# One softmax split into near keys and keys of one residue modulo 4, in a transformer block on one core

## The chip, the core and the metric

The kernel runs on one core of a Trainium2 chip. A core has TensorE (PE, matrix products into PSUM, with a weight load, PEld, ahead of each product), VectorE (DVE), ScalarE (ACT), GpSimd (POOL), and SyncE (SP), whose queue issues nearly all DMAs of this kernel. Each engine works through its own instructions in order and waits on semaphores for the others. The metric is the device time of one launch in microseconds, lower being better.

## The reference, cut to what matters

One block over 1024 tokens of 1024 channels in float32: normalization, one input projection, a gated convolution branch of width 31, an attention branch with 16 heads of 64, gates that mix both, an output projection, and a feed-forward part with a convolution of width 3. The attention is what the change rewrites:

```python
DILATION_GROUPS = ((128, 1), (512, 4), (2048, 16))
...
    for window, dilation in DILATION_GROUPS:
        o_g, lse_g = dilated_window_attention(q, k, v, slopes, window, dilation)
        outs.append(o_g)
        lses.append(lse_g)
    mix = jax.nn.softmax(jnp.stack(lses), axis=0)
    o = jnp.einsum('gbsh,gbshd->bshd', mix, jnp.stack(outs))
```

Each of the three groups attends causally within its window to keys at distances that are multiples of 1, 4 or 16, with a penalty that grows with distance (one slope a head). Mixing three softmaxes by their log-sums equals one softmax over all keys in which a key counts once for each group that holds it. So for a query only these keys have weight: all at distances 0 to 128, and beyond that those at multiples of 4 (up to 512) and of 16 (to the start). Beyond 128, every key that counts has the query's residue modulo 4.

## The kernel before, in words

Each float32 operand of a product is split into a high and a low part (`split`, lines 74 to 77: ScalarE copies the high part, VectorE subtracts it), and a product is three matmuls of the parts, or two where one operand carries both halves in its partitions.

The work runs in stages. Stage 1 (lines 197 to 342) loads x in eight tiles of 128 consecutive tokens (line 204), normalizes and transposes them, computes the two GLU halves by channel (`apad`, line 237), runs the 31-tap convolution on VectorE (`conv_branch`) beside the q, k and v products on TensorE, and spills q, k, v and the gates to DRAM. The gates' products (`gate_steps`, line 146) are a generator; a part of them covers the end of the convolution (`COVER`).

Stage 2 (lines 345 to 470) is the attention. `head` fetches one head's q, k (high and low), v and its row of the mask, all in rings of two buffers. For each block of 128 queries, `score` multiplies q with all keys up to the block's end (128 to 1024 columns), VectorE adds the mask and takes the row extreme in one operation (line 389), ScalarE takes the exponential with its row sum (391), VectorE the reciprocal (392), and GpSimd scales the row (393). `flip` transposes the probabilities by blocks of 128 keys on TensorE, and `weigh` multiplies v with them. `step` runs the scores of one half of a head beside the weighing of the half before, and `fill` pulls steps of side work from `side_work` in between, at rates set by `FILL`: a step is three matmuls of 512 columns. The side work is what is left of the gates and then the convolution branch's output product (`ya`). It has 256 + 128 such steps in all.

Stage 3 (from line 474) loads the attention's output from DRAM (`load_split(oT, do_, ...)`, line 477), multiplies it (`yb`), mixes with gates and `ya` (`merge`), and goes on to the output projection and the feed-forward part, which the change leaves alone.

The order of each engine's instructions is fixed when the program is built: a scheduler plays the program with modelled times, in the priority of the text, and writes down a sequence for each engine. On the chip the sequences stand as written.

The lines that the prediction names: 190 (transposes of x), 204, 221 to 224, 237, 261 and 322 (the end of the convolution), 374 (mask), 384 and 385 (scores), 389 to 393, 400 (transposes of probabilities), 408 and 409 (weighing), 451 to 456 (sum of both halves of the output and its store), 485 to 487 (loads of stage 3).

## Time and profile before

| | |
|---|---|
| median of 3 runs | 1814.08 us (1813.51 to 1816.09) |
| profiled execution | 1811.43 us, span 1809.6 us |
| TensorE clock granted, mean | 0.991 |
| instructions | 22474, of these 8244 matmuls |
| TensorE, VectorE, ScalarE, GpSimd busy | 98%, 73%, 43%, 11% of the span |
| DMA | 257.57 MB in 142063 packets |
| first score to last side work | 549.6 to 976.4 us |

The profile is of one execution, and its busy shares are averages over stages with different limits, so the prediction reads it by stretches. Matmuls overlap, and a busy TensorE is judged better by how far apart its products start than by their durations. A row of a group has its line, engine, operation, output and inputs, count, busy time and mean duration, then the idle time before it and what ended that. A row of a DMA has its median time from issue to landing.

### The profile page before, as it was taken

The page shows a single profiled execution, that of the slowest core. Times are in us where ns is not written, and L with a number is a line of the kernel's source. Part 1 is how long each engine was busy: PE and PEld are TensorE (multiplying, and loading weights), DVE is VectorE, ACT ScalarE, POOL GpSimd, SP SyncE. Part 2 cuts the span into 40 slices and gives each one's busy share as a digit, 9 for nine tenths or more (in the row PEclk, how much of TensorE's full clock was granted, in tenths as well). Part 3 has the DMA queues.
Part 4 walks back from the last instruction along what each step waited for, and adds up shares of the span by engine and source line. Part 5 has one row for each costly group of instructions (what it writes and reads, how often), then busy time and mean ns, then how long its engine had stood idle before and what let it go on. Part 6 is the DMA issues. An engine that isn't in the chain of part 4 may idle for free.

```text
span 1809.6 us, 22474 instructions
## 1 busy us (share of the span) xinstructions
PE 1765.8 (98%) x8244; PEld 1461.9 (81%) x8244; DVE 1318.8 (73%) x1798; ACT 771.6 (43%) x1202; POOL 195.8 (11%) x197
## 2 busy tenths in 40 slices
PE   7999999999999999999999999989999999999999
PEld 5888888888887888887888878768888888878887
DVE  5999999999735655666654543787777777789863
ACT  4111132232245656666655332545444554543441
POOL 1000133133002122222210000210000000000000
PEclk9999999999999999999999999999999999999999
DMA  5111145345549456666527543313222222389851
GB/s 203 59 47 47 41 134 163 116 134 157 157 173 246 145 158 175 180 165 179 164 70 279 169 160 133 104 48 107 80 82 81 71 95 91 116 303 335 298 180 47
DMA packets 142063, 257.57 MB, mean 142 GB/s; under 512 B 11265, under 2 KB 60545, under 8 KB 141953
## 3 DMA queue, kind: packets, MB, share of 16 engines
q1 hardware_dynamic: 141808, 255.61, 43.8%
q8 instruction: 65, 1.06, 0.3%
q10 hardware_dynamic: 144, 0.52, 0.1%
q14 instruction: 46, 0.37, 0.1%
HBM read 190.03 MB, written 66.06 MB: 142 GB/s over the span
## 4 chain that ended last, share of the span: by engine, by line
PE 53%; DMA 4%; DVE 4%; issue 1%; ACT 1%; SPq 1%; POOLq 0%; POOL 0%; DVEq 0%; ACTq 0%
PE xz L550 5%; PE xz L551 5%; PE xz L552 5%; PE dx L703 5%; PE dy L703 5%; DMA gg<-dya 2%; PE pp L400 2%; PE y L550 2%; PE y L552 2%; PE y L551 2%; PE ya L108 2%; PE ya L109 2%; PE ya L110 2%; PE o L408 2%; PE wo L126 1%; PE wo L127 1%
## 5 line engine op out<-in xcount | busy, mean ns | idle before, releaser
L253 DVE SCALAR_TENSOR_TENSOR cacc<-apad,pk,cacc 128x1024 f32<-128x1024 f32 x240 | 297.7, 1274 | 0.7
L125 PE MATMUL qkv<-hi_qkv,hT 128*128 128x512 f32 x384 | 151.8, 396 | 0.0
L127 PE MATMUL qkv<-hi_qkv,hT 128*128 128x512 f32 x384 | 150.0, 391 | 0.0
L126 PE MATMUL qkv<-lo_qkv,hT 128*128 128x512 f32 x384 | 149.4, 390 | 0.0
L389 DVE CUSTOM_DVE_ANT_0 p<-s,m 128x128 f32<-128x128 f32 (+7 forms) x128 | 95.1, 750 | 62.7 <-PE pp L400 39.0
L77 DVE TENSOR_TENSOR pl<-pp,ph 128x512 fp32r<-128x512 f32 x192 | 103.1, 549 | 49.1 <-ACT ph L76 48.6
L393 POOL TENSOR_SCALAR p<-p,st 128x128 f32<-128x128 f32 (+7 forms) x128 | 94.9, 748 | 335.5 <-DVE st L392 211.9
L76 ACT ACTIVATE ph<-pp 128x512 fp32r<-128x512 f32 x192 | 91.3, 487 | 92.2 <-PE pp L400 89.3
L649 DVE SCALAR_TENSOR_TENSOR u<-u,pk 128x1023 f32<-128x1023 f32 (+1 forms) x88 | 112.3, 1279 | 18.9 <-ACT u L647 18.5
L101 POOL TENSOR_TENSOR rs<-ss,mhalf 128x8 f32<-128x8 f32 (+1 forms) x40 | 80.3, 2010 | 353.1 <-DVE ss L100 353.0
L391 ACT ACTIVATE p<-p,st 128x128 f32<-128x128 f32 (+7 forms) x128 | 99.0, 776 | 14.6 <-DVE st L389 12.9
L108 PE MATMUL gate<-hT,hi_gt 128*128 128x512 f32 x256 | 101.8, 398 | 0.0
L109 PE MATMUL gate<-hT,hi_gt 128*128 128x512 f32 x256 | 100.8, 394 | 0.0
L110 PE MATMUL gate<-hT,lo_gt 128*128 128x512 f32 x256 | 100.3, 393 | 0.0
L400 PE MATMUL pp<-ident,p 128*128 128x128 f32 x576 | 94.4, 277 | 0.0
L127 PEld LDWEIGHTS qkv<-hi_qkv,hT 128*128 128x128 f32 x384 | 72.0, 188 | 15.3
L126 PEld LDWEIGHTS qkv<-lo_qkv,hT 128*128 128x128 f32 x384 | 72.2, 188 | 14.5 <-DVE lo_qkv L77 0.3
L125 PEld LDWEIGHTS qkv<-hi_qkv,hT 128*128 128x128 f32 x384 | 72.2, 188 | 14.0
L400 PEld LDWEIGHTS pp<-ident,p 128*128 128x128 f32 x576 | 69.5, 142 | 10.0 <-issue 0.2
L384 PE MATMUL s<-kh,q 128*128 128x512 f32 (+1 forms) x192 | 69.7, 368 | 7.3 <-DVE st L389 4.8
L408 PE MATMUL o<-ph,v 128*128 128x512 f32 x192 | 73.1, 381 | 3.6 <-ACT ph L76 1.8
L409 PE MATMUL o<-pl,v 128*128 128x512 f32 x192 | 70.5, 369 | 1.6 <-DVE pl L77 1.5
(269 smaller groups left out, 4610.4 us busy)
## 6 DMA issues: line engine op xcount, KB each, us to landing
wr<-w_down SPq DMA_DIRECT2D x45, 512.0 KB, 5.7
gr<-dff SPq DMA_DIRECT2D x62, 256.0 KB, 5.2
raw_qkv<-w_qkv SPq DMA_DIRECT2D x24, 512.0 KB, 3.9
raw_uv<-w_up SPq DMA_DIRECT2D x22, 512.0 KB, 3.3
raw_ug<-w_up SPq DMA_DIRECT2D x22, 512.0 KB, 3.3
dff<-u SPq DMA_DIRECT2D x22, 512.0 KB, 2.6
dv<-v SPq DMA_DIRECT2D x16, 512.0 KB, 3.2
raw_gt<-w_ch SPq DMA_DIRECT2D x16, 512.0 KB, 4.8
```

The source lines that it names most:

```text
L108: pe.matmul(o, hi[:, k, :], ah[:, k, :], start=(k == 0), stop=False)
L109: pe.matmul(o, hi[:, k, :], al[:, k, :], start=False, stop=False)
L110: pe.matmul(o, lo[:, k, :], ah[:, k, :], start=False, stop=(k == KT - 1))
L125: pe.matmul(ps, ah, hi[:, k % 2, :], start=(k == 0), stop=False)
L126: pe.matmul(ps, ah, lo[:, k % 2, :], start=False, stop=False)
L127: pe.matmul(ps, al, hi[:, k % 2, :], start=False, stop=(k == KT - 1))
L253: dve.scalar_tensor_tensor(out=acc, in0=a[:, j : j + T], scalar=w(j), in1=acc, op0=ALU.mult, op1=ALU.add)
L400: pe.transpose(pp[:, qb * P : (qb + 1) * P], pts[qb][:, kt * P : (kt + 1) * P], ident)
L550: pe.matmul(o, wh[:, k, :], bh[:, k, :], start=(start and k == 0), stop=False, skip_group_check=not start)
L551: pe.matmul(o, wh[:, k, :], bl[:, k, :], start=False, stop=False, skip_group_check=not start)
L552: pe.matmul(o, wl[:, k, :], bh[:, k, :], start=False, stop=(k == 3), skip_group_check=not start)
L703: pe.matmul(banks[n], a[:, c], b[:, d], start=(start and i == 0 and m == 0), stop=(stop and i == nf - 1 and m == 2), skip_group_check=True)
```

## The change

Keys are split for each query into two sets, near (the query's own block and the one before, at most 256 keys, of which those at distances up to 128 count) and far (keys of its residue modulo 4 at greater distances). Tokens of each tile of 128 stand by residue: x is loaded as 4 residues by 32 rows, and what leaves for the parts that need the order of tokens (the convolution's input, the gates, the attention's output) is written back by token with a step of four elements. In the far part, queries of one residue from four tiles form a block of 128: GpSimd copies them out of q (`qc`), and the keys of that residue are read in runs of 32 in place. `vf` holds the far values in that order, fetched by eight DMAs a head.

Each part has its own row extreme, exponential and sum (`softmax_part`). The far part's are carried through DRAM into the near part's order of rows (five DMAs), both are joined into weights, and the far weights go back through DRAM (five DMAs); GpSimd then scales all 16 pieces. The mask shrinks from 1024 to 480 columns a head, and its tile has one buffer where it had two. A head's scores all come first, and then the weighing of the head before; `FILL` is now 9 and 9 steps a head. Several pieces share one PSUM bank, and only the bank's first matmul carries the start flag (`Bank`).

```diff
-FILL = (5.5, 9.5)
+FILL = (9.0, 9.0)
+NEAR, FAR = 256, 224
...
+    def by_class(t):
+        return t.rearrange("p (t r j) -> p t r j", r=4, j=32)
+    def by_token(t):
+        return t.rearrange("p (t j r) -> p t r j", r=4, j=32)
...
+    dst = [[dr.tile([P, 16], F32, name=f"dst{i}_{a}") for a in range(2)] for i in range(H)]
...
-            act.activation(sg, gp, AF.Identity, bias=pk[:, C_GB + c : C_GB + c + 1])
+            act.activation(by_token(sg), by_class(gp), AF.Identity, bias=pk[:, C_GB + c : C_GB + c + 1])
...
-            sp.dma_start(xx, x[tt * P : (tt + 1) * P, :])
+            sp.dma_start(xx, x[tt * P : (tt + 1) * P, :].rearrange("(j r) d -> r j d", r=4))
...
-            dve.tensor_tensor(out=a[:, CW - 1 :], in0=vp, in1=sg, op=ALU.mult)
+            dve.tensor_tensor(out=by_token(a[:, CW - 1 :]), in0=by_class(vp), in1=by_class(sg), op=ALU.mult)
...
-            m = p2.tile([P, T], F32, tag="m", bufs=2, name=f"m_{h}")
+            m = p2.tile([P, 512], F32, tag="m", bufs=1, name=f"m_{h}")
+            vf = p2.tile([P, 4, 2, P], F32R, tag="vf", bufs=2, name=f"vf_{h}")
...
-            sp.dma_start(m, mask[h])
+            sp.dma_start(m[:, : NEAR + FAR], mask[h])
...
+            for a in range(4):
+                for b in range(2):
+                    fetch(vf[32 * a : 32 * a + 32, :, b, :],
+                          dv[h // 8][:, h % 8, 4 * b + a, :].rearrange("(r j) d -> j r d", r=4))
+            qc = p2.tile([P, 4, 2, 4, 32], F32R, tag="qc", bufs=1, name=f"qc_{h}")
+            for b in range(2):
+                pool.tensor_copy(qc[:, :, b], q[:, b * 512 : b * 512 + 512].rearrange("p (a r j) -> p r a j", r=4, j=32))
+            return q, qc, kh, kl, v, vf, m
...
+        def softmax_part(s, pt, m, st):
...
+        def near(h, tiles, u, st, pts):
+            q, qc, kh, kl, v, vf, m = tiles
+            s = big_ps(f"sn_{h}_{u}")
+            pt = p2.tile([P, 1024 if u else 1024 - P], F32, tag=f"pn{u}", bufs=2, name=f"pn_{h}_{u}")
+            for n in range(4):
+                if n % 2 == 0:
+                    bank = Bank()
+                i = u * 4 + n
+                nk = NEAR if i else P
+                c = slice((n + 1) * NEAR - nk, (n + 1) * NEAR)
+                k = slice((i + 1) * P - nk, (i + 1) * P)
+                bank.matmul(s[:, c], q[:, i * P : (i + 1) * P], kh[:, k], False)
+                bank.matmul(s[:, c], q[:, i * P : (i + 1) * P], kl[:, k], True)
+                pc = pt[:, c.start - (1 - u) * P : c.stop - (1 - u) * P]
+                softmax_part(s[:, c], pc, m[:, NEAR - nk : NEAR], st[:, n, u, :])
+                pts["n", i] = pc
+                yield
+        def far(h, tiles, u, st, pts):
+            q, qc, kh, kl, v, vf, m = tiles
+            s = big_ps(f"sf_{h}_{u}")
+            pt = p2.tile([P, 640], F32, tag=f"pf{u}", bufs=2, name=f"pf_{h}_{u}")
+            cls = lambda t, r, t0, t1: t.rearrange("p (t r j) -> p r t j", r=4, j=32)[:, r, t0:t1, :]
+            for b in (1, 0):
+                bank = Bank()
+                for c in range(2):
+                    r = u * 2 + c
+                    nk = FAR - (1 - b) * P
+                    s0, p0 = (c * FAR, c * FAR) if b else (512 + c * nk, 2 * FAR + c * nk)
+                    sv = s[:, s0 : s0 + nk]
+                    for kx, last in ((kh, False), (kl, True)):
+                        bank.matmul(sv.rearrange("p (t j) -> p t j", j=32), qc[:, r, b].rearrange("p a j -> p (a j)"),
+                                    cls(kx, r, 0, nk // 32), last)
+                    pc = pt[:, p0 : p0 + nk]
+                    softmax_part(sv, pc, m[:, NEAR + FAR - nk : NEAR + FAR], st[:, r, b, :])
+                    pts["f", r, b] = pc
+                    yield
+        def scores(h, tiles):
+            pts = {}
+            sts = p2.tile([P, 2, 4, 2, 2], F32, tag="sts", bufs=2, name=f"sts_{h}")
+            sf = p2.tile([P, 2, 4, 2, 2], F32, tag="sf", bufs=2, name=f"sf_{h}")[:, 0]
+            for u in range(2):
+                yield from far(h, tiles, u, sf, pts)
+            sp.dma_start(dst[h][0], sf.rearrange("p r b x -> p (r b x)"))
+            for a in range(4):
+                sp.dma_start(sts[:, 1, a, :, :],
+                             dst[h][0][32 * a : 32 * a + 32, :].rearrange("j (r b x) -> r j b x", r=4, b=2))
+            for u in range(2):
+                yield from near(h, tiles, u, sts[:, 0], pts)
+            flat = sts.rearrange("p n a b x -> p n (a b) x")
+            mx = p2.tile([P, 16], F32, tag="mx", bufs=2, name=f"mx_{h}")[:, 0:8]
+            e = p2.tile([P, 2, 8], F32, tag="ew", bufs=2, name=f"ew_{h}")
+            el = p2.tile([P, 2, 8], F32, tag="el", bufs=2, name=f"el_{h}")
+            dve.tensor_tensor(out=mx, in0=flat[:, 0, :, 0], in1=flat[:, 1, :, 0], op=ALU.min)
+            dve.tensor_tensor(out=e, in0=mx.unsqueeze(1).to_broadcast([P, 2, 8]), in1=flat[:, :, :, 0], op=ALU.subtract)
+            act.activation(e, e, AF.Exp)
+            dve.tensor_tensor(out=el, in0=e, in1=flat[:, :, :, 1], op=ALU.mult)
+            dve.tensor_tensor(out=mx, in0=el[:, 0], in1=el[:, 1], op=ALU.add)
+            dve.reciprocal(mx, mx)
+            dve.tensor_tensor(out=e, in0=e, in1=mx.unsqueeze(1).to_broadcast([P, 2, 8]), op=ALU.mult)
+            wf = p2.tile([P, 2, 4, 2], F32, tag="wf", bufs=2, name=f"wf_{h}")[:, 0]
+            sp.dma_start(dst[h][1][:, 0:8], e[:, 1])
+            for a in range(4):
+                sp.dma_start(wf[32 * a : 32 * a + 32, :, :],
+                             dst[h][1][:, 2 * a : 2 * a + 2].rearrange("(r j) b -> j r b", r=4))
+            scale = lambda pt, w: pool.tensor_scalar(pt, pt, w, 1.0, op0=ALU.mult, op1=ALU.mult)
+            wn = e[:, 0].rearrange("p (a b) -> p a b", b=2)
+            for b in range(2):
+                for a in range(4):
+                    pt = pts["n", 4 * b + a]
+                    scale(pt, wn[:, a, b : b + 1])
+                for r in range(4):
+                    scale(pts["f", r, b], wf[:, r, b : b + 1])
+            yield pts
...
+        def weigh(bank, pair, moves, last):
+            for i, (o, v, c) in enumerate(moves):
+                for n, p_ in enumerate(pair):
+                    src = p_[: v.shape[0], c]
+                    if len(o.shape) == 3:
+                        src = src.rearrange("p (t j) -> p t j", j=32)
+                    bank.matmul(o, v, src, last and n == 1 and i == len(moves) - 1)
+        def pieces(pts, v, vf, o, half):
+            nt = lambda i, k: pts["n", i][:, :P] if k < i else pts["n", i][:, -P:]
+            runs = [[(0, 0, 2), (1, 1, 2)], [(2, 2, 2), (3, 3, 1)]] if half == 0 else \
+                [[(3, 4, 1), (4, 4, 2), (5, 5, 1)], [(5, 6, 1), (6, 6, 2), (7, 7, 1)]]
+            for n, run in enumerate(runs):
+                parts, moves = [], []
+                for k, i, cnt in run:
+                    c0 = len(parts) * P
+                    i0 = (i % 4) * P
+                    moves.append((o[:, i0 : i0 + cnt * P], v[:, k, :], slice(c0, c0 + cnt * P)))
+                    parts += [nt(i + d, k) for d in range(cnt)]
+                yield f"n{half}{n}", parts, moves
+            ov = o.rearrange("p (t r j) -> p r t j", r=4, j=32)
+            for b in range(half + 1):
+                k0, k1 = b * P, (P if b < half else b * P + FAR - P)
+                parts = [pts["f", r, half][:, k0:k1] for r in range(4)]
+                moves = [(ov[:, r], vf[: k1 - k0, r, b, :], slice(r * P, (r + 1) * P)) for r in range(4)]
+                yield f"f{half}{b}", parts, moves
 
...
+        def weighing(h, pts, v, vf):
+                sum_ = p2.tile([P, 512], F32, tag="ot", bufs=2, name=f"ot_{h}_{half}")[r : r + DH, :]
+                act.activation(by_token(sum_), by_class(o[DH:P, :]), AF.Copy)
+                dve.tensor_tensor(out=by_token(sum_), in0=by_class(o[0:DH, :]), in1=by_token(sum_), op=ALU.add)
+                sp.dma_start(do_[r : r + DH, h // 2, half * 512 : half * 512 + 512], sum_)
...
+        for h in range(H + 1):
+            if h < H:
+                cur = nxt
+                for pts in scores(h, cur):
+                    fill(FILL[0] / 16)
+                if h + 1 < H:
                     nxt = head(h + 1)
-                pts = step((h, half, cur), prev)
-                prev = (h, half, pts, cur[3])
-        step(None, prev)
+            if prev is not None:
+                for _ in weighing(h - 1, *prev):
+                    fill(FILL[1] / 14)
+            prev = (pts, cur[4], cur[5])
```

More of the change, by code (lines that the diff above doesn't have):

```diff
@@ new lines, in flip @@
+        def flip(h, name, parts):
+            nk = parts[0].shape[1]
+            pp = bank_ps(f"pp_{h}_{name}")
+            for i, part in enumerate(parts):
+                pe.transpose(pp[:nk, i * P : (i + 1) * P], part, ident)
+            ph = p2.tile([P, 512], F32R, tag="ph", bufs=3, name=f"ph_{h}_{name}")
+            pl = p2.tile([P, 512], F32R, tag="pl", bufs=3, name=f"pl_{h}_{name}")
+            c = slice(0, len(parts) * P)
+            split(ph[:nk, c], pl[:nk, c], pp[:nk, c])
+            return ph, pl
@@ L419, in fill @@
                 next(filler, None)
[L421 to L429 removed]
+        def weighing(h, pts, v, vf):
+            for half in range(2):
                 o = bank_ps(f"o_{h}_{half}")
+                bank = Bank()
                 pend = []
[L432 to L442 removed]
+                todo = list(pieces(pts, v, vf, o, half))
+                for n, (name, parts, moves) in enumerate(todo):
+                    pend.append((flip(h, name, parts), moves, n == len(todo) - 1))
+                    yield
+                    if len(pend) > PEND:
+                        weigh(bank, *pend.pop(0))
+                        yield
```

93 lines of the change are left out of this document (24 added, 69 removed).

## The prediction

> **What bounds the kernel now.** I read the busy times and the chain that ended last, then the stretches of the attention stage and its two ends, then the order in time of TensorE's products there.
>
> ```profile
> span 1809.6 us, 22474 instructions
> ...
> PE 1765.8 (98%) x8244; PEld 1461.9 (81%) x8244; DVE 1318.8 (73%) x1798; ACT 771.6 (43%) x1202; POOL 195.8 (11%) x197
> ...
> PE 53%; DMA 4%; DVE 4%; issue 1%; ACT 1%; SPq 1%; POOLq 0%; POOL 0%; DVEq 0%; ACTq 0%
> ```
>
> In the stretches, the columns are start:end, length, busy time and instructions of PE, its weight loads, VectorE, ScalarE and GpSimd, TensorE's clock, the DMA share and GB/s.
>
> ```profile
> 10.00:15.00 5.00, 3.60 (x18) 2.83 (x16) 4.32 (x7) 4.43 (x8) 1.06 (x5) 1.00 1.02 419
> 50.00:496.00 446.00, 446.00 (x2037) 368.99 (x2036) 427.40 (x447) 103.88 (x137) 75.10 (x33) 1.00 0.34 106
> 549.60:976.40 426.80, 416.12 (x2206) 349.81 (x2207) 260.15 (x645) 266.28 (x556) 94.91 (x128) 0.98 0.60 175
> 950.00:977.00 27.00, 27.00 (x121) 22.36 (x120) 15.11 (x15) 18.61 (x24) 0.00 (x0) 1.00 0.95 342
> 977.00:1070.00 93.00, 90.33 (x398) 74.24 (x396) 46.59 (x65) 32.66 (x51) 0.00 (x0) 1.00 0.50 167
> ```
>
> TensorE is the bound nearly everywhere, and PE leads the chain. From the first score to the end of the side work (549.6 to 976.4) it is idle for only 10.7 us of 426.8, while VectorE and ScalarE are busy about 61% of it. So the change pays by TensorE's own time in this stage and costs wherever it makes TensorE wait. The last 27 us of the stage have no gap: side work (ya) covers the last head's output on its way through DRAM into the next stage, and the next stage loses just 2.7 us.
>
> What a product costs is the distance between starts:
>
> ```profile
> 642.69 0.23 PE L384 MATMUL s<-kh,q 128*128 128x128 f32 x1
> 642.75 0.27 PE L385 MATMUL s<-kl,q 128*128 128x128 f32 x1
> 642.86 0.45 PE L384 MATMUL s<-kh,q 128*128 128x512 f32 x1
> ...
> 643.37 0.28 PE L384 MATMUL s<-kh,q 128*128 128x256 f32 x1
> 643.49 0.28 PE L385 MATMUL s<-kl,q 128*128 128x256 f32 x1
> ...
> 643.67 0.61 PE L400 MATMUL pp<-ident,p 128*128 128x128 f32 x4
> 644.04 0.48 PE L408 MATMUL o<-ph,v 128*128 128x512 f32 x1
> 644.36 0.39 PE L409 MATMUL o<-pl,v 128*128 128x512 f32 x1
> ...
> 646.87 0.39 PE L110 MATMUL gate<-hT,lo_gt 128*128 128x512 f32 x1
> 647.10 0.39 PE L108 MATMUL gate<-hT,hi_gt 128*128 128x512 f32 x1
> ```
>
> 512 columns cost 0.23, 256 cost 0.12. Of two products of 128 the first costs 0.06 and the second 0.11, since the weights of the next one aren't in yet; a long run of them therefore costs 0.11 each. Four transposes cost 0.37, and the product behind them 0.09 more: 0.11 per transpose.
>
> **The change, part by part.** Counts are from the order of the built program, in which TensorE's sequence is fixed.
>
> *TensorE's work.* Before, a head has 24 score products (12 of 512 columns, 4 each of 384, 256 and 128), 24 weighing products of the same sizes and 36 transposes; at 0.227, 0.175, 0.118 and 0.111 that is 4.3 + 4.3 + 4.0 = 12.7 us, 203 us in 16 heads. After, it has 32 score products (14 of 256, 18 of 96 to 224), 44 weighing products (10 of 256, 34 of 128) and 27 transposes: 3.6 + 5.0 + 3.0 = 11.6 us, 186 us. Fewer columns, but in pieces too short for their weights: **-17 us**, not the third that the columns would give.
>
> *The load of x.* Each of eight tiles is now read as 4 residues by 32 rows.
>
> ```profile
> x<-x SPq DMA_DIRECT2D x8, 512.0 KB, 8.4
> ```
>
> ```profile
> 5.99 1.06 ACT L221 ACTIVATE xs<-x 128x1024 f32<-128x1024 f32 x1 [3.55 <-DMA x<-x]
> ...
> 9.41 4.03 PE L190 MATMUL tp<-ident,xs 128*128 128x128 f32 x16 [9.41 <-DVE ss L100]
> ...
> 34.15 1.91 PE L190 MATMUL tp<-ident,xs 128*128 128x128 f32 x16
> ```
>
> The packets stay 4 KB; what changes is the outermost count, 4 for 128. No row shows such a transfer. Lower bound 0: it lands as before. Upper bound: four blocks keep four of the 16 engines busy. 419 GB/s at a share of 1.02 is 26 GB/s an engine, 105 for four, 5.0 us a tile; the eighth lands about 45 (2.7 us for the start and 2.5 for the first weights in the same queue). From a tile's first touch to its transposes take 3.4 us (5.99 to 9.41), its eight transposes 1.0: done at 49.6, against 36.1 now (sixteen from 34.15). That is +13.5, and I take **+13.5**: all the transfers that reach the full rate in this trace have 64 or 128 outer rows, so the row of before is no neighbour of this one. TensorE has no gap from 50 to 496 to take it back.
> [...]
>
> *Writes by token.* The product of the GLU (8 times), the gates' copies and the head's sums write with a step of 16 bytes.
>
> ```profile
> L237 DVE TENSOR_TENSOR apad<-gluv,sg x8: 1217/1224/1226, 48.2 to 200.9; 128x1024 f32<-128x1024 f32 x8
> ...
> 487.26 1.22 DVE L261 TENSOR_TENSOR sqacc<-sqacc,csq 128x1024 f32<-128x1024 f32 x1 [1.19 <-ACT csq L260]
> ...
> 493.71 1.84 PE L322 MATMUL pss<-ones,sqacc 128*128 128x1 f32 x16
> ```
>
> No row has such a step. Bounds: nothing, and double, 8 x 1.22 = 9.8 us on VectorE, which works through the convolution without a pause (427 of 446). Its result is ready at 488.5 and used at 493.7, so 5.2 us are covered: 0 to +4.6. I take **0**, the nearest row being this operation itself. The gates' copies and sums lie on engines with 39% to spare.
> [...]
>
> *Reload of the mask.* m has one buffer now: head h+1's mask is fetched only when VectorE has read the last near scores of head h, and the first far scores need it; the third far product waits for VectorE in turn. Queued behind the waiting operation on VectorE are the splits of the probabilities, for which TensorE's weighing waits.
>
> ```profile
> L389 DVE CUSTOM_DVE_ANT_0 p<-s,m 128x256 f32<-128x256 f32 x16 | 6.7, 418 | 6.8 <-PE s L385 6.6
> ...
> L392 DVE RECIPROCAL st<-st 128x1 f32<-128x1 f32 x128 | 19.9, 157 | 16.1 <-ACT p L391 15.3
> ...
> L393 POOL TENSOR_SCALAR p<-p,st 128x256 f32<-128x256 f32 x16 | 7.7, 478 | 21.1 <-DVE st L392 15.7 <-PE o L409 5.2
> ```
>
> ```profile
> gg<-dgate SPq DMA_DIRECT2D x32, 256.0 KB, 3.6
> ...
> do<-op SPq DMA_DIRECT2D x16, 256.0 KB, 2.3
> ...
> m<-mask SPq DMA_DIRECT2D x16, 512.0 KB, 8.4
> ...
> raw_o<-do SPq DMA_DIRECT2D x8, 512.0 KB, 5.5
> ```
>
> The mask is 240 KB, nearest to gg (3.6). From the last near product: 0.7 until VectorE has read it, 0.3 for the issue, 3.6 to land, 0.5 for the first far scores (VectorE's 0.42 for 256 columns, and the hand-over), so 5.1 us. TensorE's ordered work in between, head by head, is 0.4, 14.1, 6.9, 6.9, 8.0, 8.3, 1.7, 3.4, 0.2, 13.1, 3.4, 7.1, 7.4, 2.3 and 9.9 us; six are short, by 4.7 + 3.4 + 1.7 + 4.9 + 1.7 + 2.8 = **+19 us**. With do's 2.3 it is 11, with raw_o's 5.5 it is 31. A mask ring of two, as now, hid its 8.4.
>
> *Two trips through DRAM.* Far maxima and sums go out and back (five DMAs), far weights again (five). The first trip runs beside the near scores. The second: 3.3 us from the last near product to the weights e (0.7 for the read, about as much for the exponential, six short VectorE operations at some 0.2 and a short exponential between; an estimate from the rows above), 2.3 out, 3.3 for four loads back; GpSimd meanwhile scales the near parts (8 x 0.48 = 3.8) and then four far ones of 96 columns (1.4): the first far transposes can start at 10.3. The work ordered ahead of them, with the mask's stalls, falls short by 1.6, 2.5, 1 and 1.5 in four heads: **+6** (0 to 10). SP issues some 31 DMAs a head, and one takes it 0.42 us:
>
> ```profile
> L204 SPq DMA_DIRECT2D x<-x x8: 328/423/653, 0.7 to 7.5; - x8
> ```
>
> That is 13 us of the 23.6 that a head has (TensorE's 186 and 847 side products at 0.227, in 16 heads). GpSimd's two copies of q fit in its idle 78%; exponentials double in number, which ScalarE's idle third covers.
>
> *The end of the stage.* The side work is used up before head 15's last scores: no side product stands behind them. From the last near product: weights e 3.3, trip 5.6, scaling 1.4, transposes 0.45, split 1.3, weighing 1.2, sum 1.4, store 2.3, load of half an output 3.5 (gg's 3.6 here, raw_o's 5.5 when crowded), split 2.2: 22.6 us, against 8 to 9 of TensorE's work. **+13.5** (10 to 17), where before nothing was lost.
>
> *The clock.* Waits of 1.26 and 0.71 us cost more afterwards:
>
> ```profile
> 657.53 0.33 PE L384 MATMUL s<-kh,q 128*128 128x128 f32 x1 [1.26 <-DVE st L389]
> ...
> 660.65 0.78 PE L108 MATMUL gate<-hT,hi_gt 128*128 128x512 f32 x1
> 661.22 0.63 PE L109 MATMUL gate<-hT,hi_gt 128*128 128x512 f32 x1
> 661.65 0.61 PE L110 MATMUL gate<-hT,lo_gt 128*128 128x512 f32 x1
> 662.08 0.42 PE L108 MATMUL gate<-hT,hi_gt 128*128 128x512 f32 x1
> ```
>
> Starts are 0.57, 0.43 and 0.43 apart for 0.23, 0.8 us lost. Some seven stalls and the longer last one: **+7** (2 to 10).
>
> Sum: -17 + 13.5 + 0 + 19 + 6 + 13.5 + 7 = +42 on the profiled execution's 1811.4 us (its span and 1.8 around it), 1853.4. The median shown, 1814.1, lies 2.7 above that execution, so the forecast is 1856.
>
> **The rivals.** (1) x lands as before, the rest stands: 1842.5. For it: same bytes, same packets; against it: a shape of transfer that the trace lacks. Chance 0.22. (2) Not slower: runs of short products start every 0.06, as the first of a pair does, not every 0.11. The place is TensorE; 52 short products a head, 832 in all, times 0.05 are 42 us, giving 1814. It decides at 0.06 to 0.065; with x landing as before too, it gives 1801. For it the pair at 642.69, against it the third start at 642.86 and the transposes. A like result comes if short transfers land in two microseconds and x as before: 11 for the mask, 2, 11 and 3 in place of 19, 6, 13.5 and 7 give 1824, and 1813 if those waits take in the stage's 10.7 of idle time. Chance of this side 0.22. (3) The head becomes a chain: mask, far scores in four turns between TensorE and VectorE, near scores in four, each turn about 1.0 us, 14 us at least; with a split of 0.69 between every two turns and SP's queue behind stores, near 25 a head, above the 23.6 that TensorE needs. One to two us more a head give 1872 to 1888. For it: 31 DMAs in one queue; against: VectorE 61% busy. Chance 0.13.
>
> **How the numbers follow.** The forecast's case has 0.43; its own range is 1843 to 1871. Two in ten may fall outside 1804 to 1888: the lower end takes in most of rival 2, the upper one rival 3. A measurement of this kernel can tell about 0.2% from no change. Faster comes from rival 2 with x unharmed: 0.16. Same, from rival 2: 0.06. Slower: 0.78.
>
> **What would show it.** Right: x lands at five-microsecond steps and the last tp products end near 50; far score products wait for DVE st behind a DMA m; no ya product after the last o, and a gap of ten or more before the first yb; short products 0.11 apart. Wrong: the last tp near 36; starts of 0.06 in runs of o; a stage from first score to last o under 400 us. The forecast fails most likely on x, the term without a neighbour, then on the mask.

## The result, and the profile after

The changed kernel takes 1947.93 us (median; 1940.37 to 1949.62), the kernel before on the same chip 1814.38. The ratio is 1.0727 (95% interval 1.0697 to 1.0757): slower by 134 us, where 42 were forecast, and beyond the upper end of the range (1888). The profiled execution took 1949.36 us, for a span of 1947.6, against 1809.6 before: 138.0 us to find.

First the page of the kernel after: its span, the line of PE's busy time, and the chain of waits by engine.

```profile
span 1947.6 us, 23895 instructions
...
PE 1796.1 (92%) x8548; PEld 1497.6 (77%) x8548; DVE 1309.4 (67%) x1942; ACT 799.8 (41%) x1394; POOL 228.0 (12%) x357
...
PE 72%; DMA 14%; DVE 4%; SPq 4%; issue 2%; ACT 2%; POOL 0%; POOLq 0%; DVEq 0%; ACTq 0%
```

PE's share of the span falls from 98% to 92%, DMA's share of the chain rises from 4% to 14%, SP's queue from 1% to 4%. The stretches give the place: from the first score to the first product of the next stage, from the last o to that product, and from there to the end (columns as in the prediction).

```profile
581.60:1112.20 530.60, 436.04 (x2497) 377.88 (x2495) 242.25 (x785) 286.76 (x747) 128.40 (x286) 0.87 0.57 147
1089.00:1112.20 23.20, 0.33 (x3) 0.18 (x2) 12.44 (x12) 14.95 (x17) 0.00 (x0) 0.58 0.83 298
1112.20:1947.60 835.40, 818.51 (x3604) 672.84 (x3604) 587.66 (x648) 356.17 (x447) 17.33 (x12) 0.99 0.41 141
```

The stage starts 32 us later than before (581.7 for 549.6), lasts 530.5 instead of 427.3, and what follows takes 2.6 more. What TensorE waited for in the stage (columns: waiting engine, operation and line, releaser, us in total, times, longest):

```profile
PE sf L403 <- DVE sf L413: 30.4, 10, 13.6
PE yb L109 <- DVE oT L78: 22.9, 1, 22.9
PE pp_f L502 <- POOL pf L487: 18.3, 10, 3.9
PE sn L403 <- DVE sf L413: 5.8, 2, 4.9
PE ya L109 <- ACT hi_co L77: 5.3, 1, 5.3
PE pp_n L502 <- POOL pn L487: 3.5, 3, 1.9
```

Idle time is only part of it. The next table takes each distance from one product's start to the next in the stage. A product is charged the prediction's price (0.227 us for 512 columns, 0.175 for 384, 0.118 for 256, 0.111 for fewer); what lies behind its end is idle time; the rest is put under slow clock where the product itself lasts over 1.35 times its usual duration (0.63 for 0.39 us, say), and under other where it doesn't.

| us of the stage | before | after | difference |
|---|---|---|---|
| products at their full price | 398.9 | 377.9 | -21.0 |
| idle | 10.6 | 94.6 | +84.0 |
| products at slow clock (52 before, 314 after) | 8.6 | 44.2 | +35.6 |
| other | 9.1 | 13.9 | +4.8 |

TensorE's work did shrink: the heads' own products by 17.1 us, as forecast, and another 3.9 are 17 side products that now stand ahead of the stage. Waits took the 21 four times over, and the slow clock behind them nearly twice more. Against the forecast, of the 138 us the late start of the stage takes 32 (13.5 forecast), its idle time 84 (38.5), the slow clock 35.6 (7).

### The profile page after: what moved, and what is told of

Read it like the earlier page. It is cut to its first block, busy times and chain, and to the rows that moved or that the text cites. A ratio compares the mean times of both kernels' runs of the same rounds, so it can differ in the third digit from the quotient of the medians.

```text
span 1947.6 us, 23895 instructions
## 1 busy us (share of the span) xinstructions
PE 1796.1 (92%) x8548; PEld 1497.6 (77%) x8548; DVE 1309.4 (67%) x1942; ACT 799.8 (41%) x1394; POOL 228.0 (12%) x357
## 4 chain that ended last, share of the span: by engine, by line
PE 72%; DMA 14%; DVE 4%; SPq 4%; issue 2%; ACT 2%; POOL 0%; POOLq 0%; DVEq 0%; ACTq 0%
PE xz L662 5%; PE xz L663 5%; PE xz L664 5%; PE qkv L126 4%; PE qkv L128 4%; PE qkv L127 4%; PE dy L815 4%; PE dx L815 4%; PE o L403 3%; DMA dst<-ew 2%; PE gate L109 2%; PE gate L110 2%; PE gate L111 2%; PE y L662 2%; PE y L664 2%
## 5 line engine op out<-in xcount | busy, mean ns | idle before, releaser
L413 DVE CUSTOM_DVE_ANT_0 pn<-sn,m 128x256 f32<-128x256 f32 (+1 forms) x128 | 50.0, 403 | 81.7 <-PE sn L403 81.0
L413 DVE CUSTOM_DVE_ANT_0 pf<-sf,m 128x224 f32<-128x224 f32 (+1 forms) x128 | 38.2, 321 | 83.6 <-PE sf L403 54.1
L415 ACT ACTIVATE pn<-pn,sts 128x256 f32<-128x256 f32 (+1 forms) x128 | 62.5, 489 | 73.7 <-DVE sts L413 73.2
L487 POOL TENSOR_SCALAR pn<-pn,ew 128x256 f32<-128x256 f32 (+1 forms) x128 | 59.7, 488 | 248.8 <-DVE ew L481 229.4
L415 ACT ACTIVATE pf<-pf,sf 128x224 f32<-128x224 f32 (+1 forms) x128 | 53.6, 420 | 49.1 <-DVE sf L413 45.2
L109 PE MATMUL yb<-oT,hi_ao 128*128 128x512 f32 x128 | 50.7, 396 | 22.9 <-DVE oT L78 22.9
L662 PE MATMUL xz<-h2left,hi_uv 128*128 128x512 f32 x176 | 68.7, 390 | 0.7 <-ACT hi_uv L77 0.7
L664 PE MATMUL xz<-h2left,lo_uv 128*128 128x512 f32 x176 | 68.6, 390 | 0.0
L662 PE MATMUL xz<-blk_t,hi_s3g 128*128 128x512 f32 x176 | 68.5, 389 | 0.0
L663 PE MATMUL xz<-h2left,hi_uv 128*128 128x512 f32 x176 | 68.5, 389 | 0.0
```

What stands on the lines that cost most here:

```text
L109: pe.matmul(o, hi[:, k, :], ah[:, k, :], start=(k == 0), stop=False)
L415: act.activation(pt, pt, AF.Exp, bias=st[:, 0:1], scale=-1.0, accum_out=st[:, 1:2])
L662: pe.matmul(o, wh[:, k, :], bh[:, k, :], start=(start and k == 0), stop=False, skip_group_check=not start)
L663: pe.matmul(o, wh[:, k, :], bl[:, k, :], start=False, stop=False, skip_group_check=not start)
L664: pe.matmul(o, wl[:, k, :], bh[:, k, :], start=False, stop=(k == 3), skip_group_check=not start)
```

## Experiments

The theory read from the two traces: x lands late because four engines carry it; the waits of the heads (mask, trips, the end) cost themselves and a slow clock behind them. The rivals: the load is slow for another cause; a head is one chain, in which a wait taken away comes back at the next link; SP's queue is the true cause of the waits. Differences below are between ratios to the kernel before, times its 1815 us; the changed kernel's own ratio is 1.0727. A ratio is uncertain by 0.15 to 0.35%, so a difference by 6 to 8 us. Readings of a stage are of one profiled execution each. The order of the products in the heads is laid out anew when a variant's dependences change, and line numbers shift by a few.

**The load of x.** Four DMAs a tile, one per residue, in place of one:

```diff
-            sp.dma_start(xx, x[tt * P : (tt + 1) * P, :].rearrange("(j r) d -> r j d", r=4))
+            for r in range(4):
+                sp.dma_start(xx[32 * r : 32 * r + 32, :],
+                             x[tt * P : (tt + 1) * P, :].rearrange("(j r) d -> r j d", r=4)[r])
```

> Each tile of x is loaded by four DMAs, one per residue, each 32 rows of 4 KB, in place of one DMA with four outer blocks of 32 rows. Theory A (the outermost count of four keeps four of the 16 DMA engines busy, and this is all that the load costs): the tiles land every 2 to 3 us, the first product of the queries' projection stands within 6 us of where it stood before the change (200.7 us from the span's start; 231.1 in the changed kernel), and the time falls by 25 to 30, to 1918 to 1923. Rival B (rows fetched from every fourth 4 KB are slow themselves, whatever the number of blocks): tiles still land every 5 to 6 us and the time stays within 1943 to 1953. Rival C (SP's 32 issues of 0.42 us take over, 13.4 us): the eighth tile lands near 25 and the gain is 18 to 25.

And the reverse: the kernel before with the load by residue alone.

```diff
-            sp.dma_start(xx, x[tt * P : (tt + 1) * P, :])
+            sp.dma_start(xx, x[tt * P : (tt + 1) * P, :].rearrange("(j r) d -> r j d", r=4))
```

> The kernel before, with one part of the change alone: a tile of x is loaded as four residues by 32 rows in one DMA, so tokens stand in another order and the output is not the reference's. Theory A (what TensorE loses is the lateness of the last tiles, as it had products without a gap from 20 us on): first product of the queries' projection 28 to 32 us later, time 1841 to 1849. Rival (the prediction's sum, from last transpose to last transpose): 12 to 16 later, 1825 to 1832.

Measured: four DMAs give 1912.13 us, ratio 1.0531 (1.0504 to 1.0558), 36 less; the part alone costs 28: 1842.65, ratio 1.0154 (1.0136 to 1.0172). In the traces the first product of the queries' projection stands at 200.7 before, 231.2 after, 203.1 with four DMAs, and 229.6 with the part alone. Theory A's mechanism holds on both sides, though the first time lies below its 1918 to 1923 (the last tile is touched at 25.1 with four DMAs, as rival C said, but costs TensorE only 2.4); the further 8 of the first run lie in the stage, whose products are in the changed kernel's order, and are within the scatter of single executions (1940 to 1950). The kernel after: a stretch in which x loads alone, one in which weights load beside it, the first and the last tile's squares, and the last transposes (columns of the later rows: start, duration, engine and line, operation; in brackets the idle time before it and what ended that).

```profile
22.00:28.00 6.00, 2.33 (x12) 1.96 (x11) 2.04 (x3) 1.63 (x3) 0.67 (x2) 1.00 0.26 105
40.00:46.00 6.00, 2.84 (x7) 2.22 (x8) 2.63 (x4) 2.12 (x4) 0.67 (x2) 1.00 1.00 261
```

```profile
10.82 1.06 ACT L231 ACTIVATE xs<-x 128x1024 f32<-128x1024 f32 x1 [8.41 <-DMA x<-x]
...
54.06 1.06 ACT L231 ACTIVATE xs<-x 128x1024 f32<-128x1024 f32 x1 [3.57 <-DMA x<-x]
...
64.66 1.91 PE L200 MATMUL tp<-ident,xs 128*128 128x128 f32 x16
```

The kernel before: its last tile's squares, and its first product of the GLU.

```profile
21.79 1.04 ACT L221 ACTIVATE xs<-x 128x1024 f32<-128x1024 f32 x1
```

```profile
20.18 0.80 PE L108 MATMUL glug<-hT,hi_g 128*128 128x512 f32 x1 [0.48 <-ACT hT L76]
```

The kernel before with this part alone, and the changed kernel with four DMAs a tile:

```profile
22.00:28.00 6.00, 2.24 (x10) 1.57 (x8) 2.04 (x3) 2.45 (x4) 0.67 (x2) 1.00 0.26 106
```

```profile
5.00:10.00 5.00, 0.00 (x0) 0.00 (x0) 0.15 (x1) 3.19 (x4) 0.42 (x1) 1.00 1.03 232
10.00:15.00 5.00, 3.43 (x15) 3.03 (x16) 4.02 (x6) 3.66 (x9) 1.25 (x3) 1.00 1.02 310
```

A DMA share of 0.26 at 105 GB/s is what four engines of 16 give at 26 GB/s each, the rate of one at 419 GB/s and a share of 1.02 in the kernel before. With 32 outer rows in each DMA the share is 1.03 at 232 GB/s from 5 to 10, where x loads alone too, and 1.02 at 310 from 10 to 15, with weights beside it. So both kernels whose DMAs of x have an outermost count of four show a share of 0.26 while x loads alone, and the one with 32 all 16 engines; other counts were not run.

**The mask's reload.** The far part of the mask gets two buffers of its own (768 bytes more):

```diff
-            m = p2.tile([P, 512], F32, tag="m", bufs=1, name=f"m_{h}")
+            m = p2.tile([P, NEAR], F32, tag="m", bufs=1, name=f"m_{h}")
+            mf = p2.tile([P, FAR], F32, tag="mf", bufs=2, name=f"mf_{h}")
...
-            sp.dma_start(m[:, : NEAR + FAR], mask[h])
+            sp.dma_start(mf, mask[h, :, NEAR : NEAR + FAR])
+            sp.dma_start(m, mask[h, :, :NEAR])
...
```

> The mask's far 224 columns get a tile of their own with two buffers, its near 256 columns one with one buffer, so the next head's far scores need not wait until this head's near scores are read. Theory A (each wait costs itself and a slow clock after it, and waits add up): the 30 us in which far scores waited for the reading of earlier far scores fall to under 8, some 10 us of slow clock go too, and the time falls to 1905 to 1925. Rival B (a head of the changed kernel is one chain, and the next link takes the place of the one removed): waits of the far transposes for GpSimd grow by what the far scores' waits lose, and the time stays within 1935 to 1950.

Measured: 1938.28 us, ratio 1.0661 (1.0645 to 1.0677), 12 less; rival B's range. But B's reason fails too: the far transposes' waits did not grow.

```profile
PE pp_f L504 <- POOL pf L489: 15.5, 8, 4.1
PE sf L405 <- DMA m<-mask: 12.2, 1, 12.2
...
PE sf L405 <- DVE sf L415: 7.0, 10, 1.5
```

One wait of 12.2 us stayed, at the change from head 0 to head 1, where the kernel after waits 13.6; its row names the mask, but what VectorE stood 12.8 us for in this run was the first trip. There the changed kernel's trace shows (SP's queue, then VectorE, then PE):

```profile
590.54 7.61 SPq L134 DMA_DIRECT2D vf<-dv  x8
...
600.63 0.53 SPq L465 DMA_DIRECT2D dst<-sf  x1
606.70 2.26 SPq L467 DMA_DIRECT2D sts<-dst  x4
609.06 0.42 SPq L385 DMA_DIRECT2D m<-mask  x1
```

```profile
597.67 0.42 DVE L413 CUSTOM_DVE_ANT_0 pn<-sn,m 128x256 f32<-128x256 f32 x1 [0.46 <-PE sn L403]
...
610.59 0.17 DVE L475 TENSOR_TENSOR mx<-sts 128x8 f32<-128x8 f32 x1 [12.49 <-DMA sts<-dst]
...
612.11 0.39 DVE L413 CUSTOM_DVE_ANT_0 pf<-sf,m 128x224 f32<-128x224 f32 x1 [0.49 <-DMA m<-mask]
```

```profile
612.57 0.55 PE L403 MATMUL sf<-kh,qc 128*128 128x224 f32 x1 [13.64 <-DVE sf L413]
```

The far maxima and sums were there at 594, when ScalarE ended head 0's far parts. SP was issuing the next head's eight loads of far values and reached their store at 600.6; it then stood six microseconds for its landing, and the mask, whose buffer had been free since 598, was issued behind. VectorE, which works in order, stood 12.5 us at the first operation that reads the trip, with the next head's far scores behind it; the mask itself ended only the last 0.49. So the row that names far scores waiting for VectorE held two causes, and in this instance the first trip came last. It is not the trip's alone, as the run without trips shows below.

**The trips through DRAM.** First only the wait for the second is taken away, then both trips:

```diff
-                    scale(pts["f", r, b], wf[:, r, b : b + 1])
+                    scale(pts["f", r, b], e[:, 1, 2 * r + b : 2 * r + b + 1])
```

> The far parts are scaled by the far weights as they stand before the second trip through DRAM, which are those of other tokens of the tile, so the output is not the reference's; the trip's five DMAs are still issued, and nobody waits for them. Theory A: the 18 us in which far transposes waited for GpSimd and most of the 3.5 of the near ones go, with 6 to 9 us of slow clock behind them and some 4 at the end of the stage: 1915 to 1925. Rival B (the next link, the mask, takes it over): waits of far scores grow from 30 towards 45, and the time stays at 1935 to 1950.

```diff
-            sp.dma_start(dst[h][0], sf.rearrange("p r b x -> p (r b x)"))
-            for a in range(4):
...
+            act.activation(sts[:, 1].rearrange("p a b x -> p (a b x)"), sf.rearrange("p r b x -> p (r b x)"), AF.Copy)
...
-            sp.dma_start(dst[h][1][:, 0:8], e[:, 1])
-            for a in range(4):
...
```

> Both trips are left out: the far sums and maxima and the far weights are used as they stand, which are those of other tokens, so the output is not the reference's; a copy of 16 columns on ScalarE stands for the first. This is what the exchange of tokens between the two orders costs in all. Theory D: with SP relieved of 160 issues and 80 us of waiting, and no wait of GpSimd for weights, the stage loses 50 to 65 us: 1883 to 1900. Rival (the heads are held by the split of the softmax into two parts, each with its turns between TensorE and VectorE, whatever the exchange costs): no more than the 27 us that leaving the second wait alone gave, 1918 to 1930.

Measured: 1921.23 us, ratio 1.0575 (1.0540 to 1.0611), 28 less, near theory A; and 1908.62, ratio 1.0525 (1.0504 to 1.0546), 37 less, which is between the two expectations: theory D asked for 50 to 65. The exchange costs 37 us, most of it the wait for the second trip. TensorE's waits without that wait, then TensorE's and VectorE's without both trips:

```profile
PE sf L403 <- DVE sf L413: 39.1, 12, 14.7
```

```profile
PE sf L403 <- DVE sf L413: 23.8, 7, 10.8
```

```profile
DVE pf L413 <- DMA m<-mask: 17.8, 7, 11.4
```

In the first run far scores waited more, which was rival B's reason, and the stage's idle time fell by only 9 us; its products at slow clock cost 20 us less. Why so much of the slow clock went with this wait is open. In the second, far scores still wait 10.8 us at the change from head 0 to head 1: with no trip in the queue, head 1's mask was issued at 599.7 and read from 608.9, while the DMA share was 1.03 (600 to 609). So at this change, where the DMAs are crowded, the mask and the trip are each late enough by themselves, and neither two far masks nor leaving out the trips removes the wait.

**Whose queue issues it.** The ten DMAs of the trips from GpSimd; then the eight loads of far values from ScalarE:

```diff
-            sp.dma_start(dst[h][0], sf.rearrange("p r b x -> p (r b x)"))
+            pool.dma_start(dst[h][0], sf.rearrange("p r b x -> p (r b x)"))
...
-            sp.dma_start(dst[h][1][:, 0:8], e[:, 1])
+            pool.dma_start(dst[h][1][:, 0:8], e[:, 1])
...
```

> The ten DMAs a head of the two trips through DRAM are issued by GpSimd in place of SP; nothing else is moved by hand. In the changed kernel SP, which issues in order, stands 43.5 us waiting for the first trip's store and 36.0 for the second's, and head 1's mask, whose buffer is free at 598, is issued at 609 behind them. Theory D (the waits of the far scores come from SP's queue more than from the mask's one buffer): they fall from 30 to under 12, and the time to 1910 to 1928. Rival E (a trip takes as long from either queue, and GpSimd's own waiting delays the scaling instead): far scores gain a little, waits for GpSimd's scaled parts grow from 22 to over 35, and the time is 1940 to 1960.

```diff
-                    fetch(vf[32 * a : 32 * a + 32, :, b, :],
+                    fetcha(vf[32 * a : 32 * a + 32, :, b, :],
...
+    def fetcha(dst, src):
+        act.dma_start(dst.bitcast(F32), src.bitcast(F32))
```

> The eight loads a head of the values in residue order are issued by ScalarE in place of SP, 52 us of SP's 228 us of issuing in the stage. Theory D (SP's time is scarce): 1925 to 1940. Rival (ScalarE, which issues in order too, waits for the values' buffer with exponentials and splits behind it): 1950 to 1975, with TensorE waiting for ScalarE's splits.

In the changed kernel SP waits like this for the stores of the trips in the heads (581.6 to 1069), 80 us in all:

```profile
SPq L467 <- DMA dst<-sf: 43.5, 13, 5.6
SPq L485 <- DMA dst<-ew: 36.0, 14, 4.5
```

Measured: 1954.79 us, ratio 1.0786 (1.0771 to 1.0801), 11 more; and 1949.65, ratio 1.0759 (1.0740 to 1.0777), 6 more, which the intervals don't tell from no change. Rival E's time is met by the first, though the waits for GpSimd's scaled parts grew from 22 to 30 us and not to over 35, and the second stands at the edge of its rival's. Neither gave the gain of theory D. With the trips on GpSimd's queue (TensorE's waits):

```profile
PE pp_f L502 <- POOL pf L487: 27.3, 5, 14.6
...
PE sf L403 <- DVE sf L413: 17.5, 6, 12.8
```

and with the far values' loads on ScalarE's (ScalarE's waits, then TensorE's):

```profile
ACT ot L567 <- DMA vf<-dv: 117.3, 14, 15.0
```

```profile
PE pp_f L505 <- DVE ot L568: 12.4, 6, 4.6
PE ya L109 <- ACT hi_co L77: 12.3, 1, 12.3
PE sf L406 <- DVE sf L416: 10.6, 2, 7.2
```

Far scores wait less in both, as theory D had it; but the engine that now issues waits in order as SP did, and what stands behind it is late instead. SP's queue was where the wait showed; these two moves did not remove it.

**The end of the stage.**

```diff
-FILL = (9.0, 9.0)
+FILL = (8.0, 8.0)
```

> The two shares that set how much side work is spent in a head go from 9 and 9 to 8 and 8, so that some 19 steps of three products, 13 us, are left for behind the last head. Theory A (a side product covers a wait in a head as well as at the end, every head being short of cover): the gap ahead of the first product of the next stage shrinks from 22.9 to near 10, and the heads lose about as much, so the time stays within 1938 to 1950. Rival B (most heads have cover to spare): the heads lose nothing, and the time falls by 13 to 18, to 1930 to 1935.

Measured: 1939.32 us, ratio 1.0667 (1.0651 to 1.0683), 11 less: theory A by the time, at the edge, but not by its reason. The gap falls to 5.1 us, and idle time elsewhere in the stage stays at 70 to 72 us: far scores wait more for VectorE (35.7 for 30.4), near scores less (0.9 for 5.8). What took back part of the gain is the slow clock, 50 us for 44.

```profile
PE sf L403 <- DVE sf L413: 35.7, 13, 14.8
...
PE yb L109 <- ACT hi_ao L77: 5.1, 1, 5.1
```

What fills the gap in the changed kernel is seen on ScalarE and PE:

```profile
1094.00 3.90 ACT L77 ACTIVATE oT<-raw_o 128x1024 fp32r<-128x1024 f32 x4 [3.58 <-DMA do<-ot]
...
1109.92 1.06 ACT L77 ACTIVATE oT<-raw_o 128x1024 fp32r<-128x1024 f32 x1 [1.01 <-DMA raw_o<-do]
1111.16 1.06 ACT L77 ACTIVATE hi_ao<-raw_ao 128x1024 fp32r<-128x1024 f32 x1 [0.18 <-DMA raw_ao<-w_ao]
```

```profile
1112.27 0.80 PE L109 MATMUL yb<-oT,hi_ao 128*128 128x512 f32 x1 [22.94 <-DVE oT L78]
```

The first half of the output is split by 1100. The first product then waits for its weights, which use the same four raw buffers and stand behind the whole second half in the queue, and the gates (gg) share the engines with both.

**The writes by token.** All three without the step of 16 bytes, for instance:

```diff
-            dve.tensor_tensor(out=by_token(a[:, CW - 1 :]), in0=by_class(vp), in1=by_class(sg), op=ALU.mult)
+            dve.tensor_tensor(out=a[:, CW - 1 :], in0=vp, in1=sg, op=ALU.mult)
```

> The product of the GLU, the gates' copies and the heads' sums are written in the order of residues, without the step of 16 bytes, so the output is not the reference's; TensorE's order is the same to the last product. Theory A (prediction: the slower writes lie beside other work): VectorE's product of the GLU falls from 1.98 to about 1.22 us, the head's sum from 1.08 to about 0.68, and the time stays within 3 us, 1944 to 1951. Rival (the slower writes reach the path at the convolution's end and in the heads): 1935 to 1943.

Measured: 1941.44 us, ratio 1.0716 (1.0699 to 1.0733), 2 less by the ratios and 6 by the medians, so no difference that these runs can tell from none, and none excluded up to some 8: the ratio fits theory A, the median the rival. The kernel after, then this one (fewest, median and most ns):

```profile
L247 DVE TENSOR_TENSOR apad<-gluv,sg x8: 1962/1984/2011, 78.7 to 231.7; 128x1024 f32<-128x1024 f32 x8
```

```profile
L247 DVE TENSOR_TENSOR apad<-gluv,sg x8: 1217/1226/1226, 78.7 to 231.5; 128x1024 f32<-128x1024 f32 x8
```

The first score stands at 581.7 in both: the six microseconds of VectorE in the first stage are covered.

**Together.** The edits of the load, the mask and the held-back side work, as shown above, in one kernel, and then the trips left out as well:

> Three changes of the runs before at once, output as the reference's: x by four DMAs a tile, the far part of the mask in two buffers, and shares of 8 and 8 that leave side work for the end. Against the changed kernel's 1948 they gave 36, 12 and 11 us one by one (by their ratios to the kernel before). Theory A (waits add): 1880 to 1898. Rival B (side work held back is missed in the heads, now that it would cover what the mask gave free): 1900 to 1915. Rival C (fewer waits keep the clock up, so together they give more than alone): 1860 to 1879.

> The same three, and both trips left out, with far sums and weights of other tokens, so the output is not the reference's. All that is named as a cause is gone: the load, the mask's reload, the exchange, the end. Theory A (these causes are all): idle time and slow clock of the stage fall to those of the kernel before, TensorE's 21 us of saved work show, and the time is 1793 to 1808, below the kernel before. Additive forecast from the single runs, 36 + 12 + 11 + 37 off 1948: 1852 (1842 to 1862). Rival (the two-part softmax is itself a chain of turns between TensorE, VectorE, ScalarE and GpSimd that the side work doesn't cover): 1845 to 1880, with 40 us or more of idle time left in the stage, most of it ahead of far scores and near transposes.

Measured: 1905.53 us, ratio 1.0512 (1.0486 to 1.0538), and 1853.71, ratio 1.0219 (1.0199 to 1.0240). The first is rival B by its time: beside the load, mask and side work together give 3 us, which is within the uncertainty of nothing, where one by one they gave 12 and 11. The second meets the additive sum (1852), though not by the same steps, as the trips are worth 53 here. In the stage its idle time is 41.6 us and its slow clock 29.3 in all (94.6 and 44.2 after; 10.6 and 8.6 before).

```profile
PE sn L407 <- DVE sts L417: 10.8, 2, 10.5
PE sf L407 <- DVE sf L417: 10.8, 14, 2.0
PE yb L109 <- ACT hi_ao L77: 7.2, 1, 7.2
```

Theory A is refuted as it stands: 39 us over the kernel before remain. The rival's amount is right; its place, short turns ahead of far scores, carries 10.8 of the 41.6 (14 waits), 10.5 is one late near mask, and the rest is scattered. That late mask is again head 1's: it was issued at 579.9 and landed 9.4 us later, at a DMA share of 1.05 (580 to 590). So one named cause is not wholly out, as the near part of the mask still has one buffer. With the exchange left out altogether, mending the exchange alone can't bring this kernel, in this order of work, below the kernel before; other orders or shares of side work were not run.

**The clock.** The kernel before, with one buffer for its mask (512 KB):

```diff
-            m = p2.tile([P, T], F32, tag="m", bufs=2, name=f"m_{h}")
+            m = p2.tile([P, T], F32, tag="m", bufs=1, name=f"m_{h}")
```

> The kernel before, with one part of the change alone: one buffer for the mask in place of two (here 512 KB, 8.4 us from issue to landing). It has no trips and no short products behind its waits. Theory A (TensorE's slow clock follows waits, at 0.4 us for each us of idle time, as in the changed kernel 35.6 for 84): idle time of the stage grows from 10.6 by 45 to 90 us, the products at half clock cost 0.3 to 0.5 of what it grows by, and the time is 1875 to 1945. Rival (the slow clock comes with the short products and their weight loads, not with waits): half-clock products cost no more than the 8.6 us of before, and the time grows by the idle time alone. Second rival (side work covers the reload): idle under 25, time under 1835.

Measured: 1854.82 us, ratio 1.0229 (1.0195 to 1.0264), 42 more. Idle time of the stage grows by 25.5 us (10.6 to 36.1), less than expected, so the time is below theory A's 1875 as well, with side work covering part of each reload; the cost of products at slow clock by 10.7 (8.6 to 19.3), 0.42 of it, as in the changed kernel (35.6 for 84.0). So the slow clock follows waits, in a kernel with none of the new short products, and theory A's share holds where its amount doesn't. The share is no constant: 0.21 to 0.67 in the other variants. One instance in the kernel after, a wait of 2.41 us:

```profile
677.33 0.45 PE L502 MATMUL pp_f<-ident,pf 128*96 128x128 f32 x1 [2.41 <-POOL pf L487]
677.43 0.56 PE L403 MATMUL o<-ph_n,v 128*128 128x256 f32 x1
677.79 0.41 PE L403 MATMUL o<-pl_n,v 128*128 128x256 f32 x1
678.00 0.42 PE L403 MATMUL o<-ph_n,v 128*128 128x256 f32 x1
...
682.94 0.28 PE L403 MATMUL sn<-kl,q 128*128 128x256 f32 x1
```

Starts are 0.21 apart for 0.12, and products last 0.41 for 0.28, until 682.7: 27 products, 2.6 us lost, more than the wait; the granted clock there is 0.50. The clock's records show 14 such spells in the stage. Waits of 2.27, 2.36 and 2.47 us (ended at 763, 823 and 706) are followed by one too, with 0.50 granted for 3.2 to 3.3 us in each; a wait of 0.90 us (737) is not, at 1.00 granted from 736.9 to 746. So in this stage waits of little over two microseconds are not free.

## Why the prediction was wrong

- **TensorE's work, -17.** Right: -17.1 for the heads' products at its own prices (-21.0 with the side products that left the stage), and other excess up by 4.8. Products of 128 columns start 0.11 apart in a run of them (639.80, 639.91 and 640.02 in the kernel after), so rival 2's short products are refuted; the weight loads, which the prediction gives as the reason, start 0.11 apart around its short pair too (642.69, 642.80 and 642.91 in the kernel before).
- **x, +13.5.** The mechanism was right, to the number (four engines by the share of 0.26, 105 GB/s, 5 us a tile while x loads alone); the size was not: 28 us by the part alone. The step that failed is "done at 49.6, against 36.1 now". The transposes at 34.15 were not the end of the load: the last tile was touched at 21.8, and TensorE had products without a gap from 20.2 on, which have to run in any case. And the last tile came at 54, not 45: from 40 to 46 weights loaded beside x, all 16 engines were busy (share 1.00), and at 261 GB/s each moved 16 GB/s, not 26; that this explains all of the 9 us is not shown. From touch to touch the delay is 32 us, and 28 to 31 of it reached the path. Rival 1 is refuted.
- **Writes by token, 0.** Right for the first stage, where the write costs 1.62 times as much (1.98 us for 1.22) and none of it shows. For the heads' sums, no difference could be told.
- **Reload of the mask, +19.** Part right: far scores did wait 30.4 us, and two buffers for the far mask won 12. But 13.6 of the 30.4 is one wait at head 1, behind the first trip as well as the mask. The step that failed there is "3.6 to land": without the trips the mask took some 9 us from issue to use.
- **Two trips, +6.** The largest miss among the waits: 28 for the second, 37 for both, 53 once the load, the far mask and the side work are mended, the slow clock behind the waits included. What failed is "the first trip runs beside the near scores", which at head 1 left VectorE standing 12.5 us, and the pricing of the second as if its DMAs were issued when their data was ready. SP needed 228 us for its issues in the heads and stood 80 more for the trips' landings; the prediction counted only the issues.
- **The end, +13.5.** The gap is 22.9 us, and 7.7 more are idle after the last side product. The step that failed is "load of half an output 3.5": the first product needs its weights, which are queued behind the second half. Holding side work back won only 11, and nothing to speak of with the load and the mask mended too.
- **The clock, +7.** Mis-sized five times over: 35.6 in the stage. One instance (0.8 us for a wait of 1.26) was multiplied by seven stalls; there were 18 waits of a microsecond or more, and the spell shown above cost 2.6.
- **The rivals.** Rival 3 was nearest: a head takes 31.7 us (581.7 to 1089.0 over 16). But moving DMAs off SP's queue didn't help, so the queue alone is not its cause. What remains open is the 39 us of the kernel with all four edits together: part is head 1's near mask and the slow clock; chained turns are likely for the rest, but no run isolates them.

## What to carry to other kernels

Price a wait of TensorE, where it is the bound engine, at its length and some 0.4 of it again for the clock behind it (0.2 to 0.7 in these runs), and count for each engine that works or issues in order what stands behind the waiting instruction; in the two runs that moved such instructions to another queue, the cost moved with them. When a load becomes late, compare the arrival of the last tile with the time from which the bound engine runs without a gap, not the last consumer with the last consumer. And when a DMA's outermost count falls to four and its share to 0.26, as here, try it cut into several: that alone won 28 to 36 of the 134 us here.

## What the runs showed of the hardware

- Writing with a step of 16 bytes: VectorE's product of 128x1024 from PSUM took 1.98 us for 1.22; sums of 64x512 took 1.08 for 0.68 on VectorE, and copies 1.08 for 0.59 on ScalarE.
- The last four loads of x took SP 19.0 us to issue in the kernel after, at a DMA share of 0.26 for much of that time (22 to 34 us), and 3.9 in the kernel before, at 1.02 (5 to 10 us); what held the issues is not shown.
- After the 13.6 us wait at head 1, TensorE ran at half clock for 12 us, though busy for 11.6 of them (0.51 granted from 613 to 625): in this instance short products with short waits between did not end it sooner.
